# Conditioning loads two products ahead, fourteen weight tiles, and products in block order in a two-layer decoder trunk

## The chip, the cores and the metric

The kernel runs on 1 core of one Trainium2 chip. The metric is the device time of one launch in microseconds; lower is better. The engines are TensorE (PE, matmuls, with its weight loads as PEld), VectorE (DVE), ScalarE (ACT), GpSimd (POOL) and SyncE (SP), whose queue issues the transfers.

## The reference

Two layers over x of 256 tokens by 1024 features, fp32. Each layer is a half-step SwiGLU feed-forward, a token mixer, and another half-step feed-forward: HGRN2 (a gated linear recurrence, "hg") in the first layer, a chunked causal gMLP ("gm") in the second. So there are six sub-layers: ffn0, hg, ffn1, ffn2, gm, ffn3. Each is wrapped in the same way, with shift, scale and gate computed from a vector c by one matrix product per layer (1024 by 9216):

```
def sublayer(x, fn, pre_g, post_g, shift, scale, gate, res_w):
    h = rms_norm(x, pre_g) * (1.0 + scale) + shift
    return x + res_w * gate * rms_norm(fn(h), post_g)

def swiglu(h, w_in, w_out):
    a, b = jnp.split(h @ w_in, 2, axis=-1)
    return (jax.nn.silu(a) * b) @ w_out
```

The feed-forward is 1024 to 2 x 2816 to 1024. HGRN2 makes q, f, i and g by one projection, takes logarithms of the forget gate and sums them in chunks of 64, and mixes tokens by decayed scores. gMLP multiplies one half of a GELU projection (6144 wide) with a normed, spatially mixed other half.

## The kernel before, in words

**Weights.** Every weight is streamed once. A block of 128 x 2048 fp32 arrives as two transfers of 512 KB into `raw` tiles (four of them, L40), issued on SP's queue in program order (`load`, L55). ACT casts each half to float32r (hi, L119) and DVE takes the rest (lo, L120); hi and lo are two of the twelve tiles of the pool `whl` (L41), so six blocks can be held. A product is then three matmuls (hi*hi, hi*lo, lo*hi; `mm3`, `mm3f`, `chunk2`). `next_block` (L127) takes the next block in the order of a list. The same pool lends tiles to the mixers: hg keeps eight of them for q, k, v, the gate and its output, gm keeps some for v and its tables.

**Conditioning.** The matrix for shift, scale and gate is 144 transfers of 512 KB. Each goes into one of two tiles of the pool `adap` (L43) and is followed by one DVE product with c that sums into a column of `mod` (L169, writing the product itself to a scratch tile, junkv). `pace` (L134) sets how many of them are due per weight block, and `wblock` (L121 to 124) issues them behind the block's loads. In ffn0's opening (`ring`) two of three use other tiles. hg's gate routine `gate_f` (L524) takes its work tile L from the same pool and tag (L526).

**Feed-forward stages.** ffn0 starts with eight row blocks. ffn1 to ffn3 start with a token-major projection of the first two units (`proj`, L279, matmuls L291, L292, L294), whose result is multiplied by its SiLU and transposed back for each half of the tokens (`post_tok`, L388: SiLU at L392, recorded at L79; DVE product L393; transposes "tps" L396; splits L147 and L148). Then come units of 256 hidden columns: `unit2` (L371) makes chunk a and chunk b (`chunk2`, L328 and L329) twice, with ACT copies (L377, L381) and DVE sums (L378, L382). An output unit (`out_unit`, L343; matmuls "y", L142 to L144) adds one unit's contribution to four PSUM banks, and runs two units behind. Four more PSUM banks (`acc`, L50) serve all other products in turn.

**Boundaries.** `out_last` and `tail` (L250) finish a stage: squares (L216), the factor (L218, L224), the product with the gate row G (L259, L263), the update of x (L265), and the next stage's norm (L233, transposes "npa" L239, h L243 to L248). G is broadcast from DRAM by POOL's queue (L199, L201), the only transfers that don't go through SP.

**Order.** The program is written in stages; a scheduler then orders each engine's instructions. Each engine runs its own in order. An instruction on PE can be tied behind another by `self.gate` and `paced` (L67).

Of the kernel before, what the change touches and what calls it, by code (L numbers as in the profile page):

```python
# [33 lines left out]
class Body:  # L34
    def __init__(self, ctx, tc, ins, out):
        self.ctx, self.tc, self.nc, self.out = ctx, tc, tc.nc, out
        self.d = dict(zip(_INS, ins))
        pool = lambda name, bufs, **k: ctx.enter_context(tc.tile_pool(name=name, bufs=bufs, **k))
        self.const = pool("const", 1)
        self.raw = pool("raw", 4)  # L40
        self.whl = pool("whl", 12)  # L41
        self.act = pool("act", 1)
        self.adap = pool("adap", 2)  # L43
        self.cols = pool("cols", 2)
        self.tiny = pool("tiny", 4)
# [104 lines left out]

    def ada_setup(self):
        nc = self.nc
        self.ada_next = 0
        self.pace(0, 1)
        self.mod = [self.const.tile([P, 24], F32, name=f"mod{i}") for i in range(6)]
        self.cond = self.const.tile([P, D], F32, name="cond")
        self.ring = 0

    def ada(self, upto):
        nc = self.nc  # L160
        while self.ada_next < min(upto, 144):
            i = self.ada_next
            if self.ring and i % 3:
                t = self.p4.tile([P, D], F32, tag="t4", name="ada")
            else:
                t = self.adap.tile([P, D], F32, tag="ada", name="ada")
            self.load(t, self.d["ada"][i])
            junk = self.scr.tile([P, D], BF16, tag="junkv", name="junkv")
            nc.vector.tensor_tensor_reduce(junk, t, self.cond, 1.0, 0.0, ALU.mult, ALU.add,  # L169
                                           self.mod[i // 24][:, i % 24:i % 24 + 1])  # L170
            self.ada_next += 1

    def pre_cols(self, s, k0=0, k1=KC, cols=None):
# [148 lines left out]
    def chunk2(self, w, c):  # L322

        ps = self.acc.tile([P, 2, S], F32, tag="acc", name="ups")
        mm = self.nc.tensor.matmul
        for kc in range(KC):
            u = [x[:, kc * 256 + c * P:kc * 256 + (c + 1) * P] for x in w]
            self.paced(mm(ps, u[0], self.h2[:, :, :, kc, :], start=kc == 0, stop=False))  # L328
            mm(ps[:, 1, :], u[1], self.h2[:, 0, :, kc, :], start=False, stop=kc == KC - 1)  # L329
        return ps  # L330

    def mm3f(self, o, u, h, start, stop):
        mm = self.nc.tensor.matmul
        self.paced(mm(o, u[0], h[0], start=start, stop=False))  # L334
        mm(o, u[0], h[1], start=False, stop=False)  # L335
        mm(o, u[1], h[0], start=False, stop=stop)  # L336

    def gtile(self):

# [1 line left out]
        return [g[:, i * 512:(i + 1) * 512].rearrange("p (k s) -> p k s", k=2) for i in range(2)]  # L341

    def out_unit(self, y, gT, wo, first):  # L343
        for t in range(NT):
            for h in range(2):
                for k in range(2):
                    self.out_mm(y[t][h], t, h, gT, k, wo, k, first and k == 0, False)

# [9 lines left out]
    def ffn(self, f, hT, G_fn, pre_next, nxt, bg):  # L358
        nc = self.nc
        state = {"out": 0}  # L360
        nb = self.next_block
        self.ahead = 0

        def post(pa, pb):
            sa, gT = self.t2(), self.gtile()
            self.tact(sa, pa, AF.Silu)
            nc.vector.tensor_mul(sa, sa, pb)
            self.split_ps(*gT, sa.rearrange("p (k s) -> p k s", k=2))
            return gT

        def unit2(wa, wb):  # L371

            sa, sb, gT = self.t2(), self.t2(), self.gtile()
            for c in range(2):
                sl = slice(c * S, (c + 1) * S)
                pa = self.chunk2(wa, c)
                nc.scalar.copy(sa[:, sl], pa[:, 1, :])  # L377
                nc.vector.tensor_add(sa[:, sl], sa[:, sl], pa[:, 0, :])  # L378
                self.tact(sa[:, sl], sa[:, sl], AF.Silu)
                pb = self.chunk2(wb, c)  # L380
                nc.scalar.copy(sb[:, sl], pb[:, 1, :])  # L381
                nc.vector.tensor_add(sb[:, sl], sb[:, sl], pb[:, 0, :])  # L382
                yield
            nc.vector.tensor_mul(sa, sa, sb)
            self.split_ps(*gT, sa.rearrange("p (k s) -> p k s", k=2))
            pend.append(gT)

        def post_tok(pa, pb):  # L388
            gTs = [self.gtile() for _ in range(2)]
            for t in range(NT):  # L390
                sa = self.t2()
                self.tact(sa, pa[t], AF.Silu)  # L392
                nc.vector.tensor_mul(sa, sa, pb[t])  # L393
                ps = self.acc.tile([P, 512], F32, tag="acc", name="tps")
                for k in range(4):
                    nc.tensor.transpose(ps[:, k * P:(k + 1) * P], sa[:, k * P:(k + 1) * P], self.ident)  # L396
                pv = ps.rearrange("p (u k s) -> p u k s", u=2, k=2)
                for u in range(2):
                    self.split_ps(*[g[:, :, t * P:(t + 1) * P] for g in gTs[u]], pv[:, u])
            return gTs  # L400

        def out():
            self.out_unit(y, pend.pop(0), nb(), state["out"] == 0)
            state["out"] += 1

        if f == 0:
            res = [self.acc.tile([P, 512], F32, tag="acc", name="ups") for i in range(4)]
            res += [self.yps.tile([P, 512], F32, tag=f"y{i // 2}{i % 2}", name="ups") for i in range(4)]
            res = [res[i] for i in (0, 4, 1, 5, 2, 6, 3, 7)]
            for kc in range(KC):  # L410
                self.first_h(kc)
                wb = nb()
                jobs = [(i, c, u) for i in range(8) for c in range(2) for u in range(3)]
                if kc < 7:
                    jobs.sort(key=lambda q: q[2])
                for i, c, u in jobs:
                    c0 = i * 256 + c * P
                    nc.tensor.matmul(res[i][:, c * S:(c + 1) * S], wb[u // 2][:, c0:c0 + P], hT[u % 2][:, :, kc, :],  # L418
                                     start=kc + c + u == 0, stop=kc == KC - 1 and c + u == 3)
                if kc == 6:  # L420
                    self.ahead = 1
            self.ahead, self.ring = 0, 0
            pend = [post(res[2 * i], res[2 * i + 1]) for i in range(4)]
            self.late_consts()
        else:
            wa, wb = [[nb(), nb()] for _ in range(2)]
            pend = post_tok(*self.proj(hT, [wa, wb], 512, split=True))
        y = self.y_banks()
        self.pace(bg, 25 if f == 0 else 26)
        for u in range(len(pend), 11):  # L430
            if f == 0:
                pa = self.unit(hT, nb())
# [52 lines left out]
    def hgrn(self, hT, G_fn, pre_next, nxt, bg):  # L485
        nc, tc = self.nc, self.tc
# [4 lines left out]
        nb = self.next_block  # L491
# [31 lines left out]

        def gate_f(hb, pr, z):  # L524

            L = self.adap.tile([P, 512], F32, tag="ada", name="L")  # L526
            c = slice(512 * pr, 512 * pr + 512)
            k, nk, b = kn[hb][:, c], kn[hb][:, H4:][:, c], bq[hb][:, c]
            nc.scalar.activation(L, z, AF.Abs)
# [246 lines left out]
    def gmlp(self, hT, G_fn, pre_next, nxt, bg):  # L776
        nc, tc = self.nc, self.tc
        N = 512
        st = self.const.tile([P, NT, 6, 6], F32, name="st")
        nb = self.next_block  # L780
# [8 lines left out]
            self.tact(o, o, AF.Gelu_apprx_tanh)  # L789

        v, vt = [], []
        self.pace(bg, 30, 6)
        for j in range(6):
            if j == 0:
                bbs = [bcast(self.t2(N), "gbin", N * i) for i in range(2)]
# [7 lines left out]
            for t in range(NT):  # L803
                o = v[-1][:, j % 2, t, :]
# [32 lines left out]
        pend, done = [], 0  # L837
# [244 lines left out]

# [13 lines left out]
```

## Time and profile before

| | us |
|---|---|
| median of 3 runs | 1191.47 (1190.19 to 1195.34) |
| profiled execution | 1193.24 |
| its span, first to last instruction | 1191.5 |
| PE busy | 1146.5 (96%) |
| DVE busy | 888.8 (75%) |
| ACT busy | 657.2 (55%) |
| POOL busy | 6.8 (1%) |

The mean granted clock of PE is 0.984 and the mean traffic 237 GB/s. In the rows, L with a number is the line of the kernel before; a row of a timeline gives the start, the duration, the engine, the line, the operation, what it writes from what, and in brackets the idle time just before it with what ended it. Durations of matmuls overlap, as they are pipelined: a 512-column matmul that reads 0.39 starts 0.23 us behind the last. The stages lie at about 0 to 200 (ffn0), 200 to 383 (hg), 383 to 575 (ffn1), 575 to 770 (ffn2), 770 to 990 (gm) and 990 to 1191 (ffn3).

### The profile page before, as it was taken

The numbers are of one execution on the slowest core, as the hardware profiler recorded it, in microseconds if no ns is written. First come the engines' busy times: TensorE is split into PE (matmuls) and PEld (weight loads), VectorE is DVE, ScalarE is ACT, GpSimd is POOL, SyncE is SP. The second block draws the span as 40 slices with busy tenths as digits, with TensorE's granted clock in tenths as the row PEclk, the third lists the DMA queues.
The fourth block names the chain that finished last, engine by engine and source line by source line (L and its number), as shares of the span: only waits on it lengthen the run. The fifth ranks groups of instructions, "written<-read, shape, count | busy, mean of one in ns | idle before, by whom it ended". The sixth has DMA issues, their size and how long they took to land.

```text
span 1191.5 us, 17180 instructions
## 1 busy us (share of the span) xinstructions
PE 1146.5 (96%) x6518; PEld 995.4 (84%) x6518; DVE 888.8 (75%) x1331; ACT 657.2 (55%) x1054; POOL 6.8 (1%) x16
## 2 busy tenths in 40 slices
PE   7999999997997999999999999999999999999997
PEld 6999998797895788888778888888888887888886
DVE  6997888868887887787677787657978786666652
ACT  6464446648766754456655545554754457555541
POOL 0000000000000000000000000000000000000000
PEclk9999999997999999999999999999999999999999
DMA  9899998782335777887578888537777765666640
GB/s 345 311 314 318 333 327 314 251 285 101 124 95 185 263 267 272 278 272 262 173 251 267 282 269 272 188 124 261 277 254 262 248 212 177 203 222 233 213 137 36
DMA packets 79765, 282.32 MB, mean 237 GB/s; under 512 B 9873, under 2 KB 10561, under 8 KB 79682
## 3 DMA queue, kind: packets, MB, share of 16 engines
q1 hardware_dynamic: 78626, 278.05, 68.0%
q0 software_dynamic: 1056, 3.17, 0.8%
q8 instruction: 51, 0.84, 0.3%
q14 instruction: 32, 0.26, 0.1%
HBM read 280.11 MB, written 1.07 MB: 236 GB/s over the span
## 4 chain that ended last, share of the span: by engine, by line
PE 73%; DMA 10%; DVE 8%; ACT 5%; issue 3%; SPq 0%; DVEq 0%; ACTq 0%
PE ups L328 15%; PE ups L329 8%; PE y L144 7%; PE y L142 7%; PE y L143 7%; PE ups L418 4%; DMA ada<-in_ada 4%; DMA raw<-in_wffn 4%; DVE w L120 3%; PE ups L334 3%; PE ups L336 3%; PE ups L335 3%; DMA raw<-in_whg 3%; ACT w L119 2%; PE ab L599 2%
## 5 line engine op out<-in xcount | busy, mean ns | idle before, releaser
L120 DVE TENSOR_TENSOR w<-raw,w 128x1024 fp32r<-128x1024 f32 x376 | 453.5, 1220 | 84.7 <-ACT w L119 77.5
L119 ACT CAST w<-raw 128x1024 fp32r<-128x1024 f32 x376 | 388.0, 1050 | 202.9 <-DMA raw<-in_wffn 79.4
L328 PE MATMUL ups<-h,w 128*128 128x512 f32 x864 | 303.1, 394 | 0.0
L169 DVE CUSTOM_DVE_ANT_0 junkv<-ada,cond 128x1024 bf16<-128x1024 f32 x144 | 175.8, 1221 | 92.0 <-DMA ada<-in_ada 91.5
L329 PE MATMUL ups<-h,w 128*128 128x256 f32 x864 | 242.5, 281 | 0.0
L328 PEld LDWEIGHTS ups<-h,w 128*128 128x128 f32 x864 | 162.3, 188 | 36.8
L142 PE MATMUL y<-w,t 128*128 128x512 f32 x448 | 179.4, 400 | 4.5 <-ACT t L147 4.5
L143 PE MATMUL y<-w,t 128*128 128x512 f32 x448 | 178.2, 398 | 0.0
L144 PE MATMUL y<-w,t 128*128 128x512 f32 x448 | 177.6, 397 | 0.2
L329 PEld LDWEIGHTS ups<-h,w 128*128 128x128 f32 x864 | 163.7, 190 | 0.9
L334 PE MATMUL ups<-h,w 128*128 128x256 f32 x416 | 118.3, 285 | 0.6 <-ACT w L119 0.6
L336 PE MATMUL ups<-h,w 128*128 128x256 f32 x416 | 117.8, 283 | 0.2 <-DVE w L120 0.2
L335 PE MATMUL ups<-h,w 128*128 128x256 f32 x416 | 117.6, 283 | 0.0
L142 PEld LDWEIGHTS y<-w,t 128*128 128x128 f32 x448 | 84.5, 189 | 24.1 <-ACT t L147 5.3
L144 PEld LDWEIGHTS y<-w,t 128*128 128x128 f32 x448 | 84.3, 189 | 21.0 <-DVE t L148 1.1
L143 PEld LDWEIGHTS y<-w,t 128*128 128x128 f32 x448 | 84.5, 189 | 17.9
L79 ACT ACTIVATE t<-t 128x256 f32<-128x256 f32 (+2 forms) x70 | 36.3, 523 | 97.7 <-DVE t L378 95.5
L334 PEld LDWEIGHTS ups<-h,w 128*128 128x128 f32 x416 | 79.7, 192 | 1.7 <-ACT w L119 0.8
L335 PEld LDWEIGHTS ups<-h,w 128*128 128x128 f32 x416 | 79.7, 192 | 0.8 <-issue 0.2
L336 PEld LDWEIGHTS ups<-h,w 128*128 128x128 f32 x416 | 79.7, 192 | 0.4 <-DVE w L120 0.4
L291 PE MATMUL pps<-w,h 128*128 128x512 f32 x160 | 64.4, 403 | 5.3 <-DVE h L247 5.3
L292 PE MATMUL pps<-w,h 128*128 128x512 f32 x160 | 63.8, 399 | 0.0
(199 smaller groups left out, 1435.4 us busy)
## 6 DMA issues: line engine op xcount, KB each, us to landing
raw<-in_wffn SPq DMA_DIRECT2D x264, 512.0 KB, 5.5
ada<-in_ada SPq DMA_DIRECT2D x144, 512.0 KB, 6.5
raw<-in_wgmu SPq DMA_DIRECT2D x48, 512.0 KB, 5.2
raw<-in_whg SPq DMA_DIRECT2D x40, 512.0 KB, 5.8
raw<-in_wgmv SPq DMA_DIRECT2D x24, 512.0 KB, 5.0
G<-gflat POOLq DMA_DIRECT2D x6, 512.0 KB, 5.9
t<-in_gbin SPq DMA_DIRECT2D x6, 256.0 KB, 5.2
x<-in_x SPq DMA_DIRECT2D x2, 512.0 KB, 4.0
```

The lines of the kernel that those rows point to most:

```text
L119: nc.scalar.copy(hi[:, sl], raw)
L120: nc.vector.tensor_sub(lo[:, sl], raw, hi[:, sl])
L142: self.paced(mm(ps, l[0], r[0], start=start, stop=False))
L143: mm(ps, l[0], r[1], start=False, stop=False)
L144: mm(ps, l[1], r[0], start=False, stop=stop)
L169: nc.vector.tensor_tensor_reduce(junk, t, self.cond, 1.0, 0.0, ALU.mult, ALU.add, self.mod[i // 24][:, i % 24:i % 24 + 1])
L291: mm(res[g][t], h(0, kc), u(0, kc), start=kc == 0, stop=False)
L328: self.paced(mm(ps, u[0], self.h2[:, :, :, kc, :], start=kc == 0, stop=False))
L329: mm(ps[:, 1, :], u[1], self.h2[:, 0, :, kc, :], start=False, stop=kc == KC - 1)
L334: self.paced(mm(o, u[0], h[0], start=start, stop=False))
L335: mm(o, u[0], h[1], start=False, stop=False)
L336: mm(o, u[1], h[0], start=False, stop=stop)
```

## The change

Five edits, made together.

1. `whl` has 14 tiles (seven blocks), `adap` three; L has a tile of its own (pool `lp`, one, and the scratch tile "hf", for the two halves of a gate).
2. Outside of ffn0's opening, `ada` issues the loads up to two products ahead of the product that it emits, and the product overwrites its own input.
3. In ffn1 to ffn3 `post_tok` is a generator: the first token half's transposes, chunks a and b of the first `unit2`, then the second half, then the other chunks.
4. Every output group of `out_unit` is tied behind the last matmul of the product issued before it ("block order"); the paces are 22, 23 and 27 blocks in place of 25, 26 and 30, and set ahead of the projection in ffn1 to ffn3.
5. The ring in which POOL's transfers keep their descriptors is set to 2048.

```
-        self.whl = pool("whl", 12)
+        self.whl = pool("whl", 14)
         self.act = pool("act", 1)
-        self.adap = pool("adap", 2)
+        self.adap = pool("adap", 3)
+        self.lp = pool("lp", 1)
...
         while self.ada_next < min(upto, 144):
             i = self.ada_next
-            if self.ring and i % 3:
-                t = self.p4.tile([P, D], F32, tag="t4", name="ada")
-            else:
-                t = self.adap.tile([P, D], F32, tag="ada", name="ada")
-            self.load(t, self.d["ada"][i])
-            junk = self.scr.tile([P, D], BF16, tag="junkv", name="junkv")
-            nc.vector.tensor_tensor_reduce(junk, t, self.cond, 1.0, 0.0, ALU.mult, ALU.add,
+            for j in range(len(self.ada_tiles), min(i + (1 if self.ring else 3), 144)):
+                if self.ring and j % 3:
+                    t = self.p4.tile([P, D], F32, tag="t4", name="ada")
+                else:
+                    t = self.adap.tile([P, D], F32, tag="ada", name="ada")
+                self.load(t, self.d["ada"][j])
+                self.ada_tiles.append(t)
+            t = self.ada_tiles[i]
+            nc.vector.tensor_tensor_reduce(t, t, self.cond, 1.0, 0.0, ALU.mult, ALU.add,
                                            self.mod[i // 24][:, i % 24:i % 24 + 1])
...
-            mm(ps[:, 1, :], u[1], self.h2[:, 0, :, kc, :], start=False, stop=kc == KC - 1)
+            self.last = mm(ps[:, 1, :], u[1], self.h2[:, 0, :, kc, :], start=False, stop=kc == KC - 1)
...
         for t in range(NT):
             for h in range(2):
+                self.gate = self.last
                 for k in range(2):
                     self.out_mm(y[t][h], t, h, gT, k, wo, k, first and k == 0, False)
...
         def post_tok(pa, pb):
             gTs = [self.gtile() for _ in range(2)]
+            pend.extend(gTs)
             for t in range(NT):
...
-            return gTs
+                yield
...
-            pend = post_tok(*self.proj(hT, [wa, wb], 512, split=True))
+            pend = []
+            self.pace(bg, 23)
+            tokens = post_tok(*self.proj(hT, [wa, wb], 512, split=True))
+            next(tokens)
+            steps = unit2(nb(), nb())
+            next(steps)
+            next(tokens)
         y = self.y_banks()
-        self.pace(bg, 25 if f == 0 else 26)
+        if f == 0:
+            self.pace(bg, 22)
...
             else:
-                steps = unit2(nb(), nb())
-                next(steps)
+                if u > 2:
+                    steps = unit2(nb(), nb())
+                    next(steps)
                 next(steps)
...
-            L = self.adap.tile([P, 512], F32, tag="ada", name="L")
+            L = self.lp.tile([P, 512], F32, tag="L", name="L") if pr else self.scr.tile([P, 512], F32, tag="hf", name="L")
...
-        self.pace(bg, 30, 6)
+        self.pace(bg, 27, 6)
...
-    nc = bacc.Bacc("TRN2", target_bir_lowering=False, num_devices=1)
+    nc = bacc.Bacc("TRN2", target_bir_lowering=False, num_devices=1, dynamic_dma_scratch_size=2048)
```

**SP in hg, before.** `raw` are halves of weight blocks, `ada` conditioning loads; these are the loads around the gate's projection.

```order
L56 DMA raw_2648<-in_whg 128x1024
L56 DMA raw_2652<-in_whg 128x1024
L56 DMA ada_2656<-in_ada 128x1024
L56 DMA ada_2660<-in_ada 128x1024
L56 DMA raw_2666<-in_whg 128x1024
L56 DMA raw_2670<-in_whg 128x1024
L56 DMA ada_2674<-in_ada 128x1024
L56 DMA ada_2678<-in_ada 128x1024
L56 DMA ada_2682<-in_ada 128x1024
L56 DMA raw_2827<-in_whg 128x1024
```

The same place of SP after the change:

```order
L57 DMA raw_2599<-in_whg 128x1024
L57 DMA raw_2603<-in_whg 128x1024
L57 DMA ada_2607<-in_ada 128x1024
L57 DMA ada_2610<-in_ada 128x1024
L57 DMA raw_2615<-in_whg 128x1024
L57 DMA raw_2619<-in_whg 128x1024
L57 DMA ada_2623<-in_ada 128x1024
L57 DMA ada_2626<-in_ada 128x1024
L57 DMA raw_2770<-in_whg 128x1024
```

One conditioning load less stands ahead of the next weights, and each of these loads now needs the tile of the product three loads back, where it was the product two loads back.

**DVE in the same place, before.** The L120 rows are the lo parts of the two blocks; L532 to L548 are the gate's steps; the L169 rows are the products.

```order
L120 TENSOR_TENSOR w_2665<-raw_2670,w_2664 128x1024
L169 ISA junkv_2676,mod2_105<-ada_2674,cond_109 128x1024
L169 ISA junkv_2680,mod2_105<-ada_2678,cond_109 128x1024
L532 SCALAR_TENSOR_TENSOR w_2482<-fps_2686,L_2735 128x512
L169 ISA junkv_2684,mod2_105<-ada_2682,cond_109 128x1024
L533 SCALAR_TENSOR_TENSOR w_2620<-fps_2686,L_2735 128x512
L120 TENSOR_TENSOR w_2826<-raw_2827,w_2825 128x1024
L543 SCALAR_TENSOR_TENSOR w_2482<-w_2482,loglb_2637,L_2735 128x256 x2
```

After the change:

```order
L121 TENSOR_TENSOR w_2614<-raw_2619,w_2613 128x1024
L548 SCALAR_TENSOR_TENSOR w_2437<-fps_2629,L_2678 128x512
L549 SCALAR_TENSOR_TENSOR w_2571<-fps_2629,L_2678 128x512
L173 ISA ada_2623,mod2_108<-ada_2623,cond_112 128x1024
L173 ISA ada_2626,mod2_108<-ada_2626,cond_112 128x1024
L559 SCALAR_TENSOR_TENSOR w_2437<-w_2437,loglb_2588,L_2678 128x256 x2
L121 TENSOR_TENSOR w_2769<-raw_2770,w_2768 128x1024
```

The gate's first two DVE steps come ahead of the products, two products stand between them and its next step, and the lo part of the next block comes last.

**PE in ffn2's token stage, before.** "tps" are the transposes of the two token halves, "y" output products, "ups" the chunks of the first unit.

```order
L294 MATMUL pps_5677<-w_5664,h2_5525 128x512 x4
L396 MATMUL tps_5779<-ident_110,t2_5776 128x128 x4
L142 MATMUL y00_5800<-w_6025,t4_5774 128x512
L143 MATMUL y00_5800<-w_6026,t4_5774 128x512
L142 MATMUL y01_5801<-w_6025,t4_5774 128x512
L143 MATMUL y01_5801<-w_6026,t4_5774 128x512
L396 MATMUL tps_5791<-ident_110,t2_5788 128x128 x4
L328 MATMUL ups_5835<-h2_5525,w_5804 128x512
```

After the change (each of the two chunks is sixteen matmuls long, and only its first two are shown):

```order
L299 MATMUL pps_5592<-w_5579,h2_5440 128x512 x4
L404 MATMUL tps_5694<-ident_113,t2_5691 128x128 x4
L333 MATMUL ups_5732<-h2_5440,w_5703 128x512
L334 MATMUL ups_5732<-h2_5440,w_5704 128x256
L333 MATMUL ups_5752<-h2_5440,w_5716 128x512
L334 MATMUL ups_5752<-h2_5440,w_5717 128x256
L404 MATMUL tps_5774<-ident_113,t2_5771 128x128 x4
L333 MATMUL ups_5787<-h2_5440,w_5703 128x512
```

The early y products have gone from between the two groups of transposes, and chunks a and b of the first unit have come there.

More of the change, by code (lines that the diff above doesn't have):

```diff
@@ L152, in ada_setup @@
         nc = self.nc
-        self.ada_next = 0
+        self.ada_next, self.ada_tiles = 0, []
         self.pace(0, 1)
@@ L162, in ada @@
             i = self.ada_next
-            if self.ring and i % 3:
-                t = self.p4.tile([P, D], F32, tag="t4", name="ada")
-            else:
-                t = self.adap.tile([P, D], F32, tag="ada", name="ada")
-            self.load(t, self.d["ada"][i])
-            junk = self.scr.tile([P, D], BF16, tag="junkv", name="junkv")
-            nc.vector.tensor_tensor_reduce(junk, t, self.cond, 1.0, 0.0, ALU.mult, ALU.add,
+            for j in range(len(self.ada_tiles), min(i + (1 if self.ring else 3), 144)):
[7 more added lines that the diff above has]
+            nc.vector.tensor_tensor_reduce(t, t, self.cond, 1.0, 0.0, ALU.mult, ALU.add,
                                            self.mod[i // 24][:, i % 24:i % 24 + 1])
+            self.ada_tiles[i] = None
             self.ada_next += 1
@@ L335, in mm3f @@
         mm(o, u[0], h[1], start=False, stop=False)
-        mm(o, u[1], h[0], start=False, stop=stop)
+        self.last = mm(o, u[1], h[0], start=False, stop=stop)
     def gtile(self):
```

## The prediction

> **What bounds the kernel now.** I read the page first (whole span), then the windows view (where TensorE, PE, is short of work), then the waits and the timelines of those places. The page's rows give the share of each engine, and the slices' rows the granted clock and the traffic.
>
> ```profile
> span 1191.5 us, 17180 instructions
> PE 1146.5 (96%) x6518; PEld 995.4 (84%) x6518; DVE 888.8 (75%) x1331; ACT 657.2 (55%) x1054; POOL 6.8 (1%) x16
> PEclk9999999997999999999999999999999999999999
> GB/s 345 311 314 318 333 327 314 251 285 101 124 95 185 263 267 272 278 272 262 173 251 267 282 269 272 188 124 261 277 254 262 248 212 177 203 222 233 213 137 36
> ```
>
> PE is busy 96% of the span, so work taken from other engines buys time only where PE has none. The windows view shows where (start:end, length, PE busy, PEld, DVE, ACT, POOL, granted clock, DMA share, GB/s).
>
> ```profile
> 21.00:207.00 186.00, 186.00 (x1301) 173.51 (x1301) 158.25 (x223) 95.26 (x121) 1.21 (x2) 1.00 0.91 322
> 268.00:294.00 26.00, 19.31 (x110) 18.49 (x109) 21.51 (x37) 24.70 (x48) 0.00 (x0) 0.74 0.33 116
> 273.20:280.00 6.80, 5.45 (x25) 5.45 (x26) 5.79 (x10) 6.68 (x13) 0.00 (x0) 0.50 0.64 228
> 286.90:293.70 6.80, 6.80 (x34) 6.80 (x33) 3.80 (x9) 6.00 (x16) 0.00 (x0) 0.50 0.26 84
> 412.00:416.00 4.00, 2.31 (x14) 1.51 (x13) 2.84 (x5) 2.35 (x4) 0.00 (x0) 1.00 1.02 377
> 416.00:574.00 158.00, 158.00 (x827) 134.63 (x826) 118.07 (x171) 78.60 (x127) 1.08 (x2) 1.00 0.78 267
> 606.00:616.00 10.00, 7.45 (x33) 5.76 (x32) 7.79 (x13) 4.23 (x7) 0.00 (x0) 0.83 0.96 355
> 611.10:614.50 3.40, 3.40 (x14) 2.82 (x13) 2.88 (x6) 2.44 (x4) 0.00 (x0) 0.51 1.07 372
> 1020.00:1024.00 4.00, 2.59 (x13) 1.63 (x12) 2.67 (x5) 1.93 (x4) 0.00 (x0) 1.00 1.01 377
> ```
>
> In the long middle of a feed-forward stage (21 to 207, 416 to 574) PE has no idle time at full clock: nothing that the change does there can be gained. The worst place is the recurrent mixer from 268 to 294: PE idles 26.00 - 19.31 = 6.7 us, and of its busy time (5.45 + 6.80) us ran at clock 0.50 and so held half as much work; the place loses 6.7 + 12.25 / 2 = 12.8 us. The three token stages (the 412, 606 and 1020 rows) idle 1.69 + 2.55 + 1.41 = 5.65 us, and the middle one has 3.4 us at half clock, 1.7 us more: 7.35 us. The waits view tells what the conditioning products wait for, and whom their loads hold up (SPq is SyncE's queue of transfers).
>
> ```profile
> DVE junkv L169 <- DMA ada<-in_ada: 91.5, 51, 5.4
> ACT L L529 <- DVE mod L169: 3.9, 1, 3.9
> SPq L56 <- DVE mod L169: 77.2, 42, 6.2
> ```
>
> Nearly all of the 91.5 and 77.2 us lie in the stretches where PE is full, and are hidden. What matters is what they do at the transitions.
>
> **The mixer's gate, 256 to 294.** First SyncE, then DVE, ScalarE (ACT) and PE in the timeline.
>
> ```profile
> 251.56 7.32 SPq L56 DMA_DIRECT2D ada<-in_ada  x3
> 258.97 26.85 SPq L56 DMA_DIRECT2D raw<-in_whg  x10
> 257.30 1.22 DVE L169 CUSTOM_DVE_ANT_0 junkv<-ada,cond 128x1024 bf16<-128x1024 f32 x1
> 259.87 0.60 ACT L529 ACTIVATE L<-fps 128x512 f32<-128x512 f32 x1 [3.90 <-DVE mod L169]
> 264.06 1.05 ACT L119 CAST w<-raw 128x1024 fp32r<-128x1024 f32 x1 [2.26 <-DMA raw<-in_whg]
> 270.02 0.39 PE L334 MATMUL fps<-h,w 128*128 128x256 f32 x1 [0.67 <-ACT w L119]
> 272.22 0.39 PE L336 MATMUL fps<-h,w 128*128 128x256 f32 x1 [1.69 <-DVE w L120]
> 274.55 0.58 PE L336 MATMUL fps<-h,w 128*128 128x256 f32 x1 [1.36 <-DVE w L120]
> 286.16 3.05 PE L599 MATMUL ab<-t 128*128 128x64 f32 x16 [2.97 <-DVE t L593]
> ```
>
> L, the gate's work tile, sat in the conditioning tiles' pool, so ACT stood 3.90 us until a product (the one at 257.30) had freed a tile. SyncE was held in three conditioning loads over 7.32 us, so the next weights left only at 258.97, and ACT stood another 2.26 us for them. From 264 on ACT has no slack: 24.70 of 26.00 us. The change gives L its own tiles and lets conditioning loads run on a third buffer, and there is one weight block more: both stops go, and I let the ACT chain start 3.90 + 2.26 = 6.2 us earlier. PE's 12.8 us cannot all be had, because ACT then is the limit: the gain is the 6.2, less about 0.2 for the product that now stands between two links of this chain on DVE (1.22 us, mostly under ACT's own work): **-6.0 us**. Bounds: 0 if the chain is caught elsewhere, -12.8 if PE is never late.
>
> **The token stages.** Before, PE does the transposes of the first token half, two to seven early y products, the second half's transposes and then the up-projections. Now one whole up-projection pair (a, then b) stands between. PE's rows of the first of the three stages, and the DVE and ACT steps that its new chain is made of:
>
> ```profile
> 413.76 0.50 PE L142 MATMUL y<-w,t 128*128 128x512 f32 x1 [0.83 <-ACT t L147]
> 415.35 0.66 PE L396 MATMUL tps<-ident,t 128*128 128x128 f32 x4 [0.85 <-DVE t L393]
> 421.59 0.37 ACT L381 COPY t<-ups 128x256 f32<-128x256 f32 x1 [0.77 <-PE ups L329]
> 285.28 0.62 ACT L79 ACTIVATE L<-L 128x512 f32<-128x512 f32 x1
> 414.61 0.68 DVE L393 TENSOR_TENSOR t<-t,pps 128x512 f32<-128x512 f32 x1
> 609.32 0.50 PE L142 MATMUL y<-w,t 128*128 128x512 f32 x1 [2.43 <-ACT t L147]
> ```
>
> The old waits (0.83, 0.85, 2.43) go, and two come. In the changed order ACT does the second half's SiLU only after the copy of chunk b, so once b ends there follow the copy (0.37, at 421.59), a 128x512 activation of 0.62 and the DVE product of 0.68 before the transposes: 0.4 + 0.6 + 0.7, and 0.1 for the handing over, estimated: **1.8 us** with nothing queued on PE, which is in order. And chunk b needs a PSUM bank freed by the second split of the first half's transposes, which on DVE stands behind a weight subtraction and a product: between 0 and the 2.43 us of today's worst; I take 0.7, since the seventh weight block brings the casts forward by about one block. That is 3 x (1.8 + 0.7) = 7.5 against 7.35: **0 us**. Bounds: 3 x 1.8 - 7.35 = -2, and 3 x (1.8 + 2.43 + 1.7) - 7.35 = +10.4 with a half-clock window in each. Whether a stall costs such a window is read from the trace: 1.69 us of idle (412) left the clock at 1.00, and 2.55 us (606) brought 3.4 us at 0.51. [...]
>
> **The stage boundary at 574.** DVE stands 5.40 us in front of a product whose load was issued late, and the residual update behind it is late for the next norm:
>
> ```profile
> 565.03 0.43 SPq L56 DMA_DIRECT2D ada<-in_ada  x1
> 571.66 1.23 DVE L169 CUSTOM_DVE_ANT_0 junkv<-ada,cond 128x1024 bf16<-128x1024 f32 x1 [5.40 <-DMA ada<-in_ada]
> 576.83 1.84 PE L239 MATMUL npa<-ident,xn 128*128 128x128 f32 x8 [2.05 <-DVE xn L233]
> 577.00:580.40 3.40, 3.40 (x13) 3.01 (x13) 2.41 (x4) 3.40 (x7) 0.00 (x0) 0.50 0.00 0
> 768.00:772.00 4.00, 3.92 (x22) 2.97 (x21) 2.20 (x6) 3.75 (x11) 0.00 (x0) 1.00 0.00 0
> ```
>
> PE loses 2.05 us and 3.40 / 2 = 1.7 us of half clock, 3.75 in all; the same boundary at 768 loses 0.08. In the new order two products stand in DVE's queue here, their loads still issued right behind the last weights, so the later one still lands near 571: a third of 3.75 goes, **-1.3 us** (0 to -3.75). At the boundary into the second feed-forward stage (383) a second product now precedes the split of h: it costs part of its 1.22 us, **+0.5** (0 to +3, if it has to wait for its data as this one did).
>
> **The gating mixer, 875 and 953.** Two conditioning loads come late and PE waits behind the DVE step that follows:
>
> ```profile
> 875.48 1.23 DVE L169 CUSTOM_DVE_ANT_0 junkv<-ada,cond 128x1024 bf16<-128x1024 f32 x1 [3.10 <-DMA ada<-in_ada]
> 878.30 0.71 PE L854 MATMUL vps<-w 128*128 128x128 f32 x4 [1.15 <-DVE t L861]
> 953.58 0.71 PE L854 MATMUL vps<-w 128*128 128x128 f32 x4 [0.44 <-DVE t L861]
> ```
>
> With loads two products ahead these go: 1.15 + 0.44, **-1.6 us** (0 to -1.6).
>
> **Edits at nothing.** Writing the product over its input takes no instruction more and frees junkv. [...]
>
> ```profile
> G<-gflat POOLq DMA_DIRECT2D x6, 512.0 KB, 5.9
> ```
>
> G is made before the stage's last output units, whose products on PE hide this; without that cover a late G would cost up to its 5.9 us at a boundary. The output units in block order move products among themselves inside full PE stretches. The paces (22, 23 and 27 blocks) put the same 144 products a little earlier, beside full PE work.
>
> **Sum.** The profiled execution took 1193.24 us, 1.7 around its span of 1191.5, and is 1.8 above the median of the runs (1191.47). Against it: -6.0 + 0 - 1.3 + 0.5 - 1.6 = -8.4, 1184.8; less 1.8, **1183.0 us**, 0.7% faster. What a measurement of this kernel can tell from no change is about 0.5%, 6 us (the three runs reach from 1190.19 to 1195.34).
>
> **Rivals.** *No gain in the mixer (0.27).* ACT's 24.70 of 26 us say that it is a chain of its own, and if its start is then set by PE's earlier products or by the products that still follow their loads closely, the 6.0 are lost: 1189.0. Against it: both stops carry a named releaser that the change removes. *DVE held by its products: slower (0.18).* DVE runs in order; a product hoisted ahead of a split or an update holds it until its data are there. The 91.5 us over 51 waits are 1.8 us each. In the new order nine such products stand ahead of a step that PE waits for (two in the mixer's gate chain, one at 383, three in the token stages, three at later boundaries). With 1.8 each the sum is -8.4 + 9 x 1.8 = +7.8: 1199.2. It decides from 0.9 us a place on. For it: the waits at 571 and 875. Against it: loads that are issued a product earlier. *PE never late (0.10).* All lower bounds, -12.8 - 2 - 3.75 + 0.5 - 1.6 = -19.7: 1171.8. Against it: ACT's load.
>
> **The numbers.** The forecast has 0.45. Its own spread is 1178 to 1188. The range 1172 to 1198 takes in both the large gain and most of the slower case. Faster by over 0.5% (below 1185.5): 0.38 of the forecast, 0.10 of the large gain and 0.04 of the first rival, 0.52; slower (above 1197.4): 0.15 of the second rival and 0.01 of mishaps in the forecast, 0.16; within: 0.32.
>
> **What would show it.** Right: no ACT wait for a product in the gate, L's activation right after its matmuls, PE's stops at 270 to 275 gone; PE waits of about 1.8 us ahead of the second transposes of each token stage, for the DVE product; at the boundary after the second feed-forward stage a DVE wait of several us for ada remains. Wrong: the mixer's stage as long as before, clock 0.50 in all three token stages, or DVE's wait for ada above 91.5 us with PE idle behind it.

## The result and the profile after

The changed kernel took 1203.82 us (median of 4 runs, 1202.52 to 1205.08) against 1191.57 before: ratio 1.0098, interval 1.0071 to 1.0124. It is 1% slower; 1183 us, with a range from 1172 to 1198, had been forecast. The profiled execution took 1204.75 us.

The page's first rows of the changed kernel: the span is 11.1 us longer, with the same work.

```profile
span 1202.6 us, 17085 instructions
PE 1150.3 (96%) x6518; PEld 997.1 (83%) x6518; DVE 886.8 (74%) x1331; ACT 659.3 (55%) x1054; POOL 6.8 (1%) x16
PEclk9999999998998999999999999999999999899999
```

The windows view of the changed kernel for the places that matter (start:end, length, busy time of PE, PEld, DVE, ACT, POOL, granted clock, DMA share, GB/s). They are the same places as in the windows of before, not the same number of matmuls; a wider window around them takes in PE time at full clock, which loses nothing:

```profile
262.00:292.00 30.00, 27.84 (x209) 27.47 (x208) 25.24 (x41) 28.18 (x53) 0.00 (x0) 0.89 0.32 107
409.00:420.00 11.00, 7.19 (x34) 5.65 (x33) 7.89 (x12) 5.01 (x10) 0.00 (x0) 0.84 0.98 378
572.00:580.00 8.00, 7.52 (x37) 5.71 (x36) 6.04 (x14) 7.94 (x22) 0.00 (x0) 1.00 0.20 66
580.00:600.00 20.00, 16.88 (x71) 13.25 (x70) 14.99 (x24) 12.57 (x23) 0.00 (x0) 0.91 0.63 212
608.00:619.00 11.00, 7.27 (x33) 5.76 (x32) 8.13 (x13) 4.53 (x10) 0.00 (x0) 0.84 1.01 379
876.00:886.00 10.00, 6.88 (x28) 5.33 (x27) 7.02 (x11) 4.82 (x7) 0.00 (x0) 0.83 0.97 343
1027.00:1043.00 16.00, 10.82 (x47) 8.73 (x45) 7.60 (x12) 5.22 (x12) 0.00 (x0) 0.79 0.49 183
```

Three rows of the kernel before that the prediction did not show, for the places that it has in common with these:

```profile
573.00:582.00 9.00, 6.95 (x28) 5.58 (x27) 6.83 (x12) 6.20 (x14) 0.00 (x0) 0.81 0.17 45
582.00:600.00 18.00, 17.14 (x78) 13.28 (x77) 13.91 (x23) 14.85 (x29) 0.00 (x0) 1.00 0.69 238
872.00:884.00 12.00, 10.85 (x69) 9.41 (x68) 8.53 (x14) 5.10 (x7) 0.00 (x0) 1.00 0.80 262
```

Loss of a window is its length less PE busy, plus the length times what the clock lacks of 1.00. That is rough, as it also counts the clock over time in which PE idles (in this way the mixer's gate lost 13.4 us before, and not the 12.8 of the prediction's sum), but it adds up:

| place | before | after | difference |
|---|---|---|---|
| mixer's gate (262 to 292 after) | 12.8 (the prediction's sum) | 2.2 + 3.3 = 5.5 | -7.3 |
| three token stages | 5.65 + 1.7 = 7.35 | 3.81 + 3.73 + 5.18 + 6.9 = 19.6 | +12.3 |
| boundary at 574 | 2.05 + 1.7 = 3.75 | 0.48 | -3.3 |
| projection of the third feed-forward (580 to 600) | 0.86 | 3.12 + 1.8 = 4.9 | +4.0 |
| gating mixer, 876 to 886 | 1.15 | 3.12 + 1.7 = 4.8 | +3.7 |
| sum | 25.9 | 35.3 | +9.4 of 11.1 |

So the gain that was forecast came, and more than that was lost elsewhere, above all in the token stages. The timeline of the first of them, PE first, then DVE, then ACT, in the changed kernel:

```profile
412.90 0.47 PE L333 MATMUL ups<-h,w 128*128 128x512 f32 x1 [2.13 <-DVE t L149]
419.07 0.66 PE L404 MATMUL tps<-ident,t 128*128 128x128 f32 x4 [1.69 <-DVE t L401]
409.71 1.23 DVE L121 TENSOR_TENSOR w<-raw,w 128x1024 fp32r<-128x1024 f32 x1 [0.85 <-ACT w L120]
410.86 0.42 DVE L149 TENSOR_TENSOR t<-tps,t 128x256 fp32r<-128x256 f32 x1
411.19 1.22 DVE L173 CUSTOM_DVE_ANT_0 ada<-ada,cond 128x1024 f32<-128x1024 f32 x1
412.33 0.42 DVE L149 TENSOR_TENSOR t<-tps,t 128x256 fp32r<-128x256 f32 x1
418.33 0.69 DVE L401 TENSOR_TENSOR t<-t,pps 128x512 f32<-128x512 f32 x1
408.63 1.05 ACT L120 CAST w<-raw 128x1024 fp32r<-128x1024 f32 x1 [1.31 <-DMA raw<-in_wffn]
417.43 0.37 ACT L388 COPY t<-ups 128x256 f32<-128x256 f32 x1 [2.76 <-PE ups L334]
417.69 0.60 ACT L80 ACTIVATE t<-pps 128x512 f32<-128x512 f32 x1
```

Chunk b stands 2.13 us for the second split (412.33), which is late through a cast that waited for weights (408.63), a weight subtraction and a product. When chunk b is done, ACT copies it, makes the second half's SiLU, DVE its product (418.33), and PE stands 1.69 us more. The middle stage repeats the first, with waits of 2.05 and 1.68 us. In the last stage a product has come into the second chain, at 1035.93 on DVE:

```profile
1030.69 0.47 PE L333 MATMUL ups<-h,w 128*128 128x512 f32 x1 [2.52 <-DVE t L149]
1037.81 0.66 PE L404 MATMUL tps<-ident,t 128*128 128x128 f32 x4 [2.66 <-DVE t L401]
1035.93 1.22 DVE L173 CUSTOM_DVE_ANT_0 ada<-ada,cond 128x1024 f32<-128x1024 f32 x1
```

The two other losses: at 592.88 a product without its data stands ahead of the split of h, and at 880 a DVE step of the gating mixer stands behind a weight subtraction whose weights come late.

```profile
592.88 1.23 DVE L173 CUSTOM_DVE_ANT_0 ada<-ada,cond 128x1024 f32<-128x1024 f32 x1 [2.17 <-DMA ada<-in_ada]
594.77 1.91 PE L299 MATMUL pps<-w,h 128*128 128x512 f32 x4 [1.84 <-DVE h L253]
877.90 1.04 ACT L120 CAST w<-raw 128x1024 fp32r<-128x1024 f32 x1 [3.88 <-DMA raw<-in_wgmu]
878.98 1.23 DVE L121 TENSOR_TENSOR w<-raw,w 128x1024 fp32r<-128x1024 f32 x1 [3.48 <-ACT w L120]
880.65 0.71 PE L870 MATMUL vps<-w 128*128 128x128 f32 x4 [3.12 <-DVE t L877]
```

In the waits view DVE's wait for conditioning data has gone from 91.5 to 59.0 us, and SyncE's for products from 77.2 to 50.1. Shorter waits there did not make PE faster. Nor is most of it due to the loads two products ahead: without them e13 has 59.4 and 50.7 us, and e4 75.4 and 41.9.

```profile
DVE ada L173 <- DMA ada<-in_ada: 59.0, 30, 4.2
SPq L57 <- DVE mod L173: 50.1, 30, 6.6
```

### The profile page after: what moved, and what is told of

Read it like the earlier page. It is cut to its first block, busy times and chain, and to the rows that moved or that the text cites. A ratio compares the mean times of both kernels' runs of the same rounds, so it can differ in the third digit from the quotient of the medians.

```text
span 1202.6 us, 17085 instructions
## 1 busy us (share of the span) xinstructions
PE 1150.3 (96%) x6518; PEld 997.1 (83%) x6518; DVE 886.8 (74%) x1331; ACT 659.3 (55%) x1054; POOL 6.8 (1%) x16
## 3 DMA queue, kind: packets, MB, share of 16 engines
HBM read 280.11 MB, written 1.07 MB: 234 GB/s over the span
## 4 chain that ended last, share of the span: by engine, by line
PE 73%; DVE 9%; DMA 8%; ACT 7%; issue 3%; SPq 0%; DVEq 0%; ACTq 0%
PE ups L333 16%; PE ups L334 8%; PE y L143 7%; PE y L144 7%; PE y L145 7%; PE ups L426 4%; PE ups L339 4%; PE ups L341 4%; PE ups L340 4%; DVE w L121 3%; DMA raw<-in_wffn 2%; DMA raw<-in_whg 2%; ACT w L120 2%; DMA ada<-in_ada 2%; PE pps L296 1%
## 5 line engine op out<-in xcount | busy, mean ns | idle before, releaser
L120 ACT CAST w<-raw 128x1024 fp32r<-128x1024 f32 x376 | 386.2, 1050 | 196.6 <-DMA raw<-in_wffn 63.1
L333 PE MATMUL ups<-h,w 128*128 128x512 f32 x864 | 308.5, 400 | 6.7 <-DVE t L149 6.7
L334 PE MATMUL ups<-h,w 128*128 128x256 f32 x864 | 244.3, 283 | 0.0
L173 DVE CUSTOM_DVE_ANT_0 ada<-ada,cond 128x1024 f32<-128x1024 f32 x144 | 174.2, 1220 | 59.0 <-DMA ada<-in_ada 59.0
L333 PEld LDWEIGHTS ups<-h,w 128*128 128x128 f32 x864 | 164.4, 190 | 45.4 <-issue 7.6
L334 PEld LDWEIGHTS ups<-h,w 128*128 128x128 f32 x864 | 165.8, 192 | 0.9
```

What stands on the lines that cost most here:

```text
L120: nc.scalar.copy(hi[:, sl], raw)
L173: nc.vector.tensor_tensor_reduce(t, t, self.cond, 1.0, 0.0, ALU.mult, ALU.add, self.mod[i // 24][:, i % 24:i % 24 + 1])
L334: self.last = mm(ps[:, 1, :], u[1], self.h2[:, 0, :, kc, :], start=False, stop=kc == KC - 1)
```

## The experiments

Each run is set against runs of the kernel before on the same chip; their median went from 1191.6 to 1195.9 from one group of runs to the next, so the ratios count.

| run | what it is | median, us | ratio and interval |
|---|---|---|---|
| changed kernel | all edits | 1203.82 | 1.0098 (1.0071 to 1.0124) |
| e1 | changed, generator undone | 1192.44 | 1.0003 (0.9972 to 1.0034) |
| e5 | changed, block order undone | 1190.49 | 0.9988 (0.9966 to 1.0009) |
| e7 | changed, both undone | 1191.27 | 0.9953 (0.9938 to 0.9968) |
| e8 | changed, SiLU and product ahead | 1186.57 | 0.9913 (0.9896 to 0.9930) |
| e12 | e8 without block order | 1183.87 | 0.9923 (0.9903 to 0.9944) |
| e13 | e8, loads at their own product | 1181.23 | 0.9904 (0.9879 to 0.9929) |
| e2 | before, generator alone | 1191.05 | 1.0001 (0.9982 to 1.0020) |
| e6 | before, block order alone | 1201.44 | 1.0047 (1.0025 to 1.0070) |
| e4 | before, all memory edits | 1185.15 | 0.9937 (0.9913 to 0.9961) |
| e9 | before, L's tiles alone | 1196.56 | 1.0011 (0.9993 to 1.0029) |
| e10 | e9 and fourteen weight tiles | 1194.52 | 1.0019 (0.9997 to 1.0041) |
| e11 | e9 and the third conditioning tile | 1180.41 | 0.9896 (0.9877 to 0.9914) |
| e16 | third conditioning tile alone | 1185.92 | 0.9941 (0.9918 to 0.9964) |
| e14 | e11 and e8's token order, no block order | 1172.61 | 0.9832 (0.9783 to 0.9881) |
| e15 | e14 and block order | 1173.68 | 0.9835 (0.9793 to 0.9877) |

All but e2 and e6 have the smaller descriptor ring. e9, which has it with little else, is no different from the kernel before (1.0011). That the added tiles need it, for its room, no run shows.

### The token stages: e1, e2, e5, e6, e7

e1 makes the two halves' transposes one after the other again:

```
-            tokens = post_tok(*self.proj(hT, [wa, wb], 512, split=True))
-            next(tokens)
-            steps = unit2(nb(), nb())
-            next(steps)
-            next(tokens)
+            for _ in post_tok(*self.proj(hT, [wa, wb], 512, split=True)):
+                pass
```

> The changed kernel with the token stages' generator undone: both token halves are transposed back to back, then chunk a and chunk b; everything else as changed, block order too. Theory T (the 20.2 us that PE loses in the three token stages, against 9.3 before, come from the two waits that the new order puts around chunk b): PE then waits once per stage, for the second half's DVE product, about 1 us, so the stages lose 3 to 6 us and the time is 1187 to 1191. Rival R (conditioning products placed ahead of due DVE steps hold PE, wherever the tokens stand): the products only move, and the time stays at 1200 to 1205.

Measured 1192.44, just above theory T's range; by the ratios (1.0003 against 1.0098) it is 0.94% below the changed kernel. Rival R is out for the token stages: the code of the products stays as it is, and the loss goes with the generator. PE's one wait per stage is 0.78, 1.34 and 3.69 us.

e2 puts the generator alone, as in the diff of the change, on the kernel before.

> The kernel before with the generator alone (edit 3), without block order. Theory T in its first form (the order of the transposes alone makes the loss): 1199 to 1203. Theory T2 (the generator loses because block order forbids the output products that would fill the wait): ten y products now stand between chunk b and the second transposes, 2.3 us of work over a chain of 1.8 us, and the time is 1188 to 1194. Rival R: 1191, as no load or tile has moved.

Measured 1.0001: the generator by itself costs nothing. The first form of T falls, and T2 stands; R had the same number here, so this run does not speak against R.

e5 takes block order out of the changed kernel:

```
         for t in range(NT):
             for h in range(2):
-                self.gate = self.last
                 for k in range(2):
```

> The changed kernel without block order (the tie in the output units is taken out). T2: the wait after chunk b is filled by y products, some 2.5 us in each of three stages and the half-clock windows go, 1192 to 1197; T in its first form and R: 1202 to 1205.

Measured 0.9988 (1190.49), a little below T2's range. In the first token stage PE waits once and for 1.07 us, ahead of chunk b (1.07 and 1.23 in the other two); the second transposes, with y products ahead of them, have no wait at all:

```profile
416.45 0.47 PE L333 MATMUL ups<-h,w 128*128 128x512 f32 x1 [1.07 <-DVE t L149]
421.41 0.60 PE L403 MATMUL tps<-ident,t 128*128 128x128 f32 x4
```

e7 has both undone (e1's and e5's edits), and e6 has block order alone on the kernel before (`self.last` kept, the output groups tied to it).

> The changed kernel with both the token generator and block order undone; memory edits, loads two products ahead and paces stay. With the changed kernel (both, 1203.8), the generator undone (1192.4) and block order undone (1190.5) it completes a square. Theory T2 (the loss is the pair's: the second transposes wait for a chain with nothing allowed beside it): 1185 to 1191, so that each of the two alone costs only a few us. Rival A (the costs add: 11.4 and 13.3): 1179.

> The kernel before with block order alone. T2: without the generator the transposes come back to back and block order costs little, 1190 to 1195. Rival A (block order costs 13 us by itself): 1202 to 1206.

Measured 0.9953 and 1.0047. The square reads: neither 0.9953, generator alone +0.35%, block order alone +0.50%, both +1.45%, so 0.6% (7 us) come from the pair alone. The four intervals together leave about 0.5% of doubt on these 0.6%, so rival A's pure sum is only just out. My T2 was too simple as well: block order alone does cost, 0.5% both on the changed kernel and on the one before, where 1190 to 1195 had been expected. e6's timeline of the first token stage shows how: with the y products tied back, PE stands 3.94 us between the transposes of the two halves, while DVE holds the second half's product behind a weight subtraction that waits for its cast.

```profile
414.92 0.66 PE L397 MATMUL tps<-ident,t 128*128 128x128 f32 x4 [3.94 <-DVE t L394]
413.04 1.23 DVE L120 TENSOR_TENSOR w<-raw,w 128x1024 fp32r<-128x1024 f32 x1 [2.81 <-ACT w L119]
414.19 0.68 DVE L394 TENSOR_TENSOR t<-t,pps 128x512 f32<-128x512 f32 x1
```

### The chain itself: e8, e12, e13

e8 leaves block order and the place of the chunks, and makes the second half's SiLU and product before the first half's transposes are emitted:

```
+            sas = [self.t2() for _ in range(NT)]
             for t in range(NT):
-                sa = self.t2()
-                self.tact(sa, pa[t], AF.Silu)
-                nc.vector.tensor_mul(sa, sa, pb[t])
+                self.tact(sas[t], pa[t], AF.Silu)
+                nc.vector.tensor_mul(sas[t], sas[t], pb[t])
+            for t in range(NT):
+                sa = sas[t]
```

> The changed kernel, with the SiLU and the product of the second token half made ahead of the first half's transposes, so that the second transposes wait for nothing made after chunk b; block order and the place of the chunks stay. T2: the waits ahead of the second transposes (about 1.7, 1.7 and 2.7 us, with half-clock time behind them) go, and only chunk b's wait for its bank stays: 1194 to 1199. If block order costs the time in some other place: 1202 to 1205.

Measured 0.9913 (1186.57), better than the 1194 to 1199 expected: the wait that T2 names went, and I had the size too small. Not only the wait for the second transposes went, but chunk b's wait as well, and the half-clock time with them. The windows view of e8 over the three stages:

```profile
400.00:416.00 16.00, 16.00 (x85) 13.64 (x84) 15.13 (x20) 10.54 (x15) 0.00 (x0) 1.00 0.87 312
600.00:616.00 16.00, 16.00 (x95) 14.00 (x94) 13.58 (x22) 9.29 (x17) 0.00 (x0) 1.00 1.00 373
1010.00:1026.00 16.00, 15.70 (x92) 13.60 (x91) 11.88 (x18) 9.37 (x18) 0.00 (x0) 1.00 0.72 247
```

PE idles 0.3 us in all three, where it lost 19.6. That chunk b no longer waits fits the four PSUM banks of `acc`: the projection fills all four, and in e8 the two of the second half are read, and so free, before chunk b needs one. No run changes the number of banks or shows them one by one, so this part is argued only.

e12 is e8 without the line `self.gate = self.last`; e13 is e8 with each load at its own product (`min(i + 1, 144)` in the loop of `ada`).

> The version with the second half's SiLU and product ahead (ratio 0.9913, token stages almost free of loss), without block order. If block order was only harmless there: 0.989 to 0.993. If it helps once the chain is gone (without it y products go between the transposes and wait for their splits, as in the kernel before): 0.994 to 0.998.

> The same version with block order, and each conditioning load issued at its own product (three tiles stay). If the loads two products ahead are worth something: 0.994 to 0.998, with DVE's wait for ada back from 50 us to 75 or more. If three tiles do it alone: 0.990 to 0.993.

Measured 0.9923 and 0.9904, both inside e8's interval: once the chain is gone, block order neither helps nor costs, and the loads two products ahead are worth nothing that can be measured. In e13 DVE's wait for conditioning data is 59.4 us against 50.0 in e8, and not the 75 that I had named as the sign of the loads being needed.

### The memory edits: e4, e9, e10, e11, e16

e4 has the memory edits of the change on the kernel before, and nothing else of it (pools of 14, 3 and 1, L's tiles, products over their input, the ring). e9 has L's tiles (and the ring), e10 adds the weight tiles, e11 adds the conditioning tile to e9; e16 has the conditioning tile without L's:

```
-        self.adap = pool("adap", 2)
+        self.adap = pool("adap", 3)
```

> The kernel before with the memory edits alone: fourteen weight tiles, three conditioning tiles, tiles of its own for L, products over their input, the small descriptor ring; loads at their own product, no block order, tokens and paces as before. Theory M (the mixer's gate gains from L's own tiles and the deeper weights): the stretch from 268 to 294 gains its 8 us here too, 1182 to 1186. Rival: the gain there needs the loads two products ahead, 1189 to 1193.

> The kernel before with L in tiles of its own alone (and the smaller descriptor ring, which makes the room); twelve weight tiles, two conditioning tiles. Theory M1 (ACT's 3.9 us stop for a product was the mixer's loss): 1184 to 1188, as with all memory edits. Theory M2 (the seventh weight block and the third conditioning tile make the gain): 1189 to 1193.

> The kernel before with L's own tiles and fourteen weight tiles (and the small ring); two conditioning tiles, and the product's junk tile as before. With all memory edits the ratio was 0.9937, with L's tiles alone 1.0011. Theory W (the seventh weight block makes the gain, as the mixer itself takes eight of the tiles and leaves three blocks in place of two): 0.992 to 0.996. Theory C (the third conditioning tile makes it, as SyncE is no longer held in front of weights): 0.999 to 1.002.

> The kernel before with L's own tiles and a third conditioning tile; twelve weight tiles. Theory W: 0.999 to 1.002. Theory C: 0.992 to 0.996.

> The kernel before with a third conditioning tile alone (and the small ring); L stays in that pool. L's tiles alone gave 1.0011, L's tiles and the third tile 0.9896. If the third tile is the gain by itself, as L and two loads then have a place each: 0.988 to 0.992. If both are needed (L takes a tile, and ACT still waits for a product): 0.996 to 1.001.

e4 measured 0.9937 (1185.15): theory M's number holds, and the mixer's gain needs no load ahead. M's reason does not hold: of the parts, L's tiles alone give 1.0011 and with fourteen weight tiles 1.0019; with the third conditioning tile they give 0.9896, better than the 0.992 to 0.996 expected, and the third tile alone 0.9941. So the third tile gives over half of the gain by itself, the two weight tiles give none of it, and L's tiles add 0.45% once the third tile is there. Each of my two theories for e16 missed: the truth lies between them. In e9 ACT no longer waits for a product, and SyncE still spends 8.36 us in front of the weights. PE stands 4.38 us for a cast of those weights:

```profile
249.63 8.36 SPq L57 DMA_DIRECT2D ada<-in_ada  x3
258.08 41.98 SPq L57 DMA_DIRECT2D raw<-in_whg  x12
276.46 0.39 PE L335 MATMUL fps<-h,w 128*128 128x256 f32 x1 [4.38 <-ACT w L120]
275.37 3.89 ACT L120 CAST w<-raw 128x1024 fp32r<-128x1024 f32 x4
```

ACT is not idle ahead of this cast. The four transfers at 258.08 had left by 260.2, and no weight transfer of the stretch took over 8.9 us, so the weights were there well before 275. What PE waits for is a cast that stands behind the gate's own steps in ACT's order.

In e11 SyncE goes to the same weights at 247.04, 11 us earlier, and the cast of the last two of these four tiles stands at 261.57, ahead of the gate's next steps. SyncE's waits for products over the whole kernel fall from 77.2 to 31.8 us, and the gate's stretch has 2.7 us of idle PE at full clock:

```profile
240.56 6.39 SPq L57 DMA_DIRECT2D ada<-in_ada  x3
247.04 48.11 SPq L57 DMA_DIRECT2D raw<-in_whg  x14
261.57 2.00 ACT L120 CAST w<-raw 128x1024 fp32r<-128x1024 f32 x2
SPq L57 <- DVE mod L170: 31.8, 22, 5.1
262.00:300.00 38.00, 35.34 (x278) 33.66 (x277) 35.66 (x58) 35.18 (x65) 1.07 (x2) 1.00 0.37 125
```

In e16, L still in the pool, ACT's wait ahead of L is 2.27 us, and for a DVE step in place of a product:

```profile
250.57 0.60 ACT L529 ACTIVATE L<-fps 128x512 f32<-128x512 f32 x1 [2.27 <-DVE log1mlb L479]
```

The two weight tiles have a price that I had overlooked. e10, which has them without the loads ahead, has a product without its data ahead of the split of h at 593.91, as the changed kernel has at 592.88; PE stands 1.28 and 1.18 us there:

```profile
593.91 1.23 DVE L170 CUSTOM_DVE_ANT_0 junkv<-ada,cond 128x1024 bf16<-128x1024 f32 x1 [1.51 <-DMA ada<-in_ada]
595.80 1.20 PE L295 MATMUL pps<-w,h 128*128 128x512 f32 x4 [1.18 <-DVE h L249]
```

e4 has the same stop (2.12 us at 592.08), and e9 and e11, with twelve tiles, do not have it there. e4, which is e11 with the two tiles and the product over its input, has 0.9937 against 0.9896. That difference is barely clear of the noise, and no run takes the two edits apart, but the stop at this place comes with the tiles.

### A version that beats both: e14, e15

e14 joins e11 with e8's token order on twelve weight tiles, old paces, loads at their product and no block order; e15 adds block order.

> L's own tiles and the third conditioning tile, with the token generator and the second half's SiLU and product ahead; no block order, loads at their product, twelve weight tiles, old paces. The token stages still lost 11.7 us of the 58.7 with the third tile: most of that should go, ratio 0.980 to 0.985. If the fourteen tiles or the loads two ahead were needed for it: 0.988 to 0.992.

> The same with block order. With the chain gone block order costs nothing: within 0.3% of the run without it. If it costs by itself as on the kernel before (0.5%): 0.985 to 0.990.

Measured 0.9832 (1172.61) and 0.9835 (1173.68), as expected: 1.7% faster than the kernel before and 2.6% faster than the changed one. e15 differs from e13 in the two weight tiles, the paces and the product over its input, and is 0.7% faster (0.9835 against 0.9904, with about 0.5% of doubt): these edits together cost time here, and which of them costs how much was not tried. The token stages of e14 in the windows view:

```profile
393.00:410.00 17.00, 17.00 (x91) 14.42 (x90) 15.50 (x20) 10.61 (x16) 0.00 (x0) 1.00 0.77 271
580.00:600.00 20.00, 20.00 (x105) 16.91 (x104) 15.63 (x21) 12.19 (x21) 0.00 (x0) 1.00 0.70 253
1000.00:1020.00 20.00, 19.54 (x115) 17.09 (x114) 14.77 (x22) 11.63 (x21) 0.00 (x0) 1.00 0.80 270
```

## Why the prediction was wrong

**The token stages are the step that failed.** It was put at 3 x (1.8 + 0.7) = 7.5 against 7.35, "0 us", and measured +12.3. The first of its two waits, the chain of copy, SiLU and product, was sized rightly in two stages and 0.9 us short in the third, where a conditioning product came into it: 1.69, 1.68 and 2.66 us for 1.8. (The 0.1 for the handing over stood on no row; 1.69 is hardly more than the steps' own 1.67.) The wait of chunk b was taken as 0.7, "since the seventh weight block brings the casts forward", between 0 and 2.43: it measured 2.13, 2.05 and 2.52, the upper end. The casts did not come forward, as the weights themselves were late: DMA share 0.98 and 1.01 in the 409 and 608 windows, as full as before (1.02 and 0.96), and a cast that waits 1.31 us for its data. And the price of the clock was left at nothing, though the middle stage before had 3.4 us at 0.51: the changed kernel has four stretches of 3.41 us at clock 0.50, from 414.08, 612.05, 1031.89 and 1038.72. The +12.3 lie even above the bound of +10.4. One of the prediction's own signs of being wrong, clock 0.50 in all three token stages, came.

**Block order was costed at nothing, and that was wrong.** "The output units in block order move products among themselves inside full PE stretches" overlooked the one place where PE is not full: it was y products that filled the token stages' waits before, and block order takes them away (e6: 0.5% alone, e5: 1.1% in company).

**The mixer's gate: right, for half of the reasons.** -6.0 was forecast and about -7.3 measured. ACT's stop for L's tile was a true wait (it ended with the product at 258.56, not with the one at 257.30 that I named), but taking it away alone gave nothing (e9). PE's stop went with the third tile, and SyncE's hold in front of the weights with it (e11, e16). In e9 PE meets the stop as a cast that comes late in ACT's order, which I had not seen; that SyncE's hold sets this place is argued, not shown. The seventh weight block gave none of it (e10), which I had counted in.

**The boundary at 574: right sign, too small.** -1.3 forecast, -3.3 measured: the product that stood 5.40 us for its data, and was to land near 571 still, stands 0.46 us, at 569.63. The +0.5 at 383 lies within what the windows can tell.

**The projection at 594: left out.** +4.0 measured, and no term of the sum had it; only the rival of held products spoke of such places. A stop of this kind came with the two weight tiles alone (e10), which were counted as pure gain.

**The gating mixer: wrong.** -1.6 forecast, +3.7 measured at 876. The product's own wait went, as said, and the 0.44 us at 953 too, but the mixer's step at 880 then stood behind a weight subtraction whose data came late (878.98): weight transfers took up to 10.0 us there from issue to landing, against 6.3 in the kernel before. e8, which keeps order, paces and loads, stands 1.74 us there and keeps its clock, so it moves with what happens before; its cause was not settled.

**The rivals.** "DVE held by its products" came closest in time, with 1199.2, and named only part of the mechanism. A product is in the way in the rows at 411.19, 592.88 and 1035.93, and at 609.29 in the middle stage. In the token stages e1 and e8 lose the loss without touching the products' code; three products of 1.22 us lie in the six waits there, so at most 3.7 us of the waits' 12.7 are theirs, and no run moves them alone. At 592.88 the rival is right: e1 and e8 keep that stop, with 2.08 and 1.63 us. "No gain in the mixer" and "PE never late" did not come.

Still open: what the paces and the product over its input do, each alone, which was not tried, and the loss at 876.

## What to carry to other kernels

Before an order is tied down, ask which work fills the waits today, for it may be the work that is tied: block order cost nothing once the wait was gone (e8 0.9913, e12 0.9923), and 0.5% to 1.1% while it was there (e6, e5). When a step is moved between two halves of a job, emit the short chain of the second half ahead of it, not behind (e8: 0.9913 against 1.0098). And where a queue serves two streams, give the one that waits for compute one more buffer before the other gets more: one conditioning tile of 4 KB per partition gave what two weight tiles did not (with L's tiles 0.9896 against 1.0019), and those brought a stop of their own (1.18 us in e10).

## What the runs showed that I had not expected

The clock fell to half after a stop shorter than the half-clock stretch that followed it. In the changed kernel 2.13 us of idle ahead of 412.90 were followed by 3.41 us at clock 0.50, in which the pairs of chunk b's matmuls (L333, L334) start 0.64 us apart, against 0.35 at clock 1.00:

```profile
414.08:417.49 3.41, 3.31 (x11) 2.42 (x10) 2.41 (x4) 0.48 (x2) 0.00 (x0) 0.50 1.00 386
```

In e11 a stop of 2.12 us, nearly all the idle time of its stretch, left the clock at 1.00:

```profile
593.88 0.50 PE L143 MATMUL y<-w,t 128*128 128x512 f32 x1 [2.12 <-ACT t L148]
588.00:598.00 10.00, 7.76 (x39) 6.05 (x38) 8.28 (x15) 5.22 (x9) 0.00 (x0) 1.00 0.90 307
```

So of two stops of 2.1 us one was followed by a half-clock stretch and the other was not, and what decides it no run here shows. A stretch of 3.41 us at 0.50 is counted here as 3.41 / 2 = 1.7 us lost; by the pace of those pairs, 0.35 against 0.64, it is 1.5.
